# A narrow first slot and a wide second one in an eight-expert layer

## The chip, the cores and the metric

One core of one Trainium2 chip runs the whole program. The metric is device time in microseconds; the kernel before takes 1734.12 us, the median of three runs (1733.98 to 1734.18).

## The reference

Two layers of a diffusion backbone over 256 latent tokens and 256 context tokens, 1024 channels, float32. Layer 0 mixes tokens with a gated chunk MLP and ends with a dense SwiGLU; layer 1 has windowed attention and ends with a mixture of experts. What the change touches is the last of these:

```
logits = xt @ w_router                       # 256 tokens, 8 experts
top_v, top_i = top_k(logits, 2)
gates = sum(one_hot(top_i) * softmax(top_v))
for e in range(8):
    y += gates[:, e:e+1] * ((silu(xt @ w_gate[e]) * (xt @ w_up[e])) @ w_down[e])
```

Each expert has w_gate and w_up of 1024 by 3584 and w_down of 3584 by 1024. The kernel computes an expert only for the tokens that chose it: 512 choices over 8 experts, 64 each on average. The output is the latent stream after a final RMSNorm.

## The kernel before, in words

Layer 0, the attention and the second layer's projections take the first 814 us or so. In the mixture of experts the kernel goes through eight **slots** in a fixed order (`MODES`, line 78). A slot has a mode that sets how many tokens it holds and how PE works on them:

- **L** (wide): 128 places. Weights are split into a high and a low fp32r part and each product is three matmuls (`mm3`, lines 231 to 234): high by high, high by low, low by high. The high part is a cast on ACT (line 168), the low part a subtraction on DVE (line 169), both in `split`.
- **S** (narrow): 64 places. Weights are used raw, as float32; the tokens are the stationary operand, 64 columns wide, so that two matmuls stand side by side on the array (`columns`, line 1500 on; the matmul is line 1504).
- **M** (middle): 96 places in three parts of 32, raw weights, four matmuls side by side (line 1504 too).

Slot 0 always holds expert 0 (its weights are addressed before routing is known); the others are ranked by their token counts, the smallest to the S slots and the largest to the remaining L slot (`SLOTRANK`, and `gating`, line 1313 on). If an expert has more tokens than its slot has places, a block under `tc.If(over > 0)` at the end runs all eight experts again, as L slots, for what is left over.

A slot's weights come in 42 **units** of 1 MiB, in the order of `expert_units`: for four chunks of hidden columns (1024, 1024, 1024, 512) the gate units, the up units, and then the down units of the chunk before, so that a slot's last down units stand among the first chunk of the next slot. `chunk` does gate, SiLU on ACT (line 1685), up, and the product of the two on DVE (line 1688); the next chunk's gate transposes that product (line 1541 for a wide slot, 1555 for a raw one) for its down matmuls.

SP issues all loads in program order (line 179). Each unit has a named buffer, and a load waits until that buffer's previous unit is no longer needed: for a raw unit until PE has read it, for a unit of an L slot until it is split. Nine units go early into tiles that are free before the layer's end (`sg`/`at`, and `ORDER`); then `FILLS` names the next buffers, issued around the attention's output projection, and `stages` (line 1133 on) yields the rest in a cycle: `RAW`, `yh`, `FIRSTS`. `side1` and `yh` drop out of the cycle after unit 40 (`YHU`), because they are needed for the sum of the experts' outputs and for a wide slot's scatter. The split halves go into five tiles in turn, three called `wd` and two of the four called `w` (`Halves.half`); `Halves.take` splits up to five halves (two and a half units) ahead of PE. Only after the last L unit do the three `wd` tiles join the cycle as buffers for raw units.

Beside the matmuls there are small steps, one for each unit taken (`extras`): the routing's `gating`, the gather of the next slot's tokens (`gather` for L, line 1388; `gather_raw`, line 1424), their scatter matrix (`back_raw`, line 1437), and `combine`, which adds a finished slot to the sum (lines 1606 and 1630). The first slot's gather runs before the first chunk, in an order written out by hand. For a wide first slot it alternates DVE and ACT and splits the tokens too (lines 1394 to 1409).

Of the kernel before, what the change touches and what calls it, by code (L numbers as in the profile page):

```python
# [8 lines left out]
def _quiet(msg, *args, **kwargs):  # L9
# [6 lines left out]
F32 = mybir.dt.float32  # L16
F32R = mybir.dt.float32r
I32 = mybir.dt.int32
AF = mybir.ActivationFunctionType
OP = mybir.AluOpType  # L20
# [3 lines left out]
P = 128  # L24
# [12 lines left out]
UNIT = 2048  # L37
# [15 lines left out]
LOOK = 2  # L53
NHALF = 5
HB = 5
FIRSTS = ('wst',) * 3 + ('xgb0', 'side0', 'wx', 'wst3', 'hx', 'side1', 'xgb1')
FILLS = 'wst wst hx0 wst xgb0 side0 wx wst3 hx1 side1'
LH = 5
RAW = ('wsx', 'wst5', 'hc', 'wst2', 'wst4')
ORDER = ('xgb0', 'xgb1', 'wsx', 'wst5', 'hc', 'wst2', 'wst4', 'yh')  # L60
PLACE = ('xgb', 'wst2', 'wst4', 'wst5', 'sg', 'at', 'yh')
TACT = 0, 2
# [8 lines left out]
BEGIN = "v a a n00 w0 s1 c t3 t2 m00 s1 a q3 a q2 W1 f n10 a n01 n11 b m10 a a n21 m01 s1 s1 a n20 n30 n31 a m11 a s1 m21 n41 a n40 m31 a w1 n51 m20 m30 s1 s1 n50 a m40 a n60 s1 s1 a n61 m41 m51 a m50 m60 m61 n70 n71 m71 m70"  # L71
START = {mybir.EngineType.PE, mybir.EngineType.SP}
WARM = 4, 4
YHU = 40
GY = 2
TMM = (3,)

MODES = "LSLMSMMS"
PARTS = {"S": (64, 1), "M": (32, 3)}
SLOTCAP = [P if m == "L" else PARTS[m][0] * PARTS[m][1] for m in MODES]  # L80
SLOTRANK = [-1] + [sum(MODES[1:].count(x) for x in "SML"[:"SML".index(m)]) + MODES[1:s + 1].count(m) - 1
                   for s, m in enumerate(MODES) if s]

# [48 lines left out]
def body(tc, nc, I, out, dbg=None):  # L132
    ctxs = []

    def pool(**kw):
        return tc.tile_pool(**kw)

    V, A, PE = nc.vector, nc.scalar, nc.tensor
# [3 lines left out]
    with top:  # L142
        con = top.enter_context(pool(name="con", bufs=1))
        psp = top.enter_context(pool(name="psum", bufs=1, space=PSUM))
        wst = top.enter_context(pool(name="wst", bufs=3))
        hpool = tc.tile_pool(name="hpool", bufs=1, side="right")
        hp = hpool.__enter__()
        cur = {}
# [3 lines left out]
        def s2t(dt=F32):  # L152
            return ph.tile([P, 512], dt, name="s2", bufs=S2)

        def wtile():
            return ph.tile([P, UNIT], F32R, name="w", bufs=4)
# [4 lines left out]
        def mm_ps(dt=F32):  # L161
            return psp.tile([P, 512], dt, name="mm", bufs=6)

        def tp_ps(dt=F32):
            return psp.tile([P, 512], dt, name="tp", bufs=2)
# [71 lines left out]
        ph = top.enter_context(pool(name="all", bufs=1))  # L237
# [56 lines left out]
        hx = [ph.tile([P, 4, 256], F32, name=f"hx{i}", bufs=1) for i in range(2)]  # L294
        hc = ph.tile([P, DT, 256], F32, name="hc", bufs=1)
# [94 lines left out]
        G = [[con.tile([P, DT, 2], F32, name=f"G{l}{n}") for n in range(2)] for l in range(2)]  # L390
# [128 lines left out]
        def mod(l, i, d, s):  # L519
            return modT[l][:, 8 * i + d, s:s + 1]  # L520
# [131 lines left out]
        first = ada_first()  # L652
# [201 lines left out]
        for g in range(7):  # L854
# [15 lines left out]
            for which in ("g", "u"):  # L870
                if g == 0 and which == "g":
                    u = []
                    ps = []
# [17 lines left out]
                for fh in range(2):  # L891
                    u = stream.take(2)
                    feed(FEED.get((g, which, fh), 1))
                    for f2 in range(2):
                        ps = mm_ps()
# [190 lines left out]
        def expert_units(exs):  # L1086
            last = None
            for ex in exs:
                c0 = 0
                for w in CH:  # L1090
                    k = 2 * 1024 // w
                    for which in ("gate", "up"):
                        for r0 in range(0, D, k * P):
                            yield ex, (which, r0, k, c0, w), (k, w)
                    if last is not None:
                        yield from down_units(*last)
                    last = ex, c0, w
                    c0 += w
            yield from down_units(*last)
# [14 lines left out]

        order = [Expert(m, s, None, None if s else 0) for s, m in enumerate(MODES)]
        first_units = list(expert_units(order))
        units = list(first_units)
        early = {n: mp.tile([P, SIZES.get(n, UNIT)], F32, name=n, bufs=1) for n in PLACE}
# [4 lines left out]
        def source(u):  # L1123
            ex, what, shape = u
            return ex.slice(*what), shape
# [6 lines left out]

        def stages():
            i = len(loaded)
            split_ends = max(j for j, u in enumerate(units) if u[0].mode == "L")
            for n in FIRSTS[FIRSTS.index("side1") + 1:]:
                i += 1
                yield n
            while True:
                for n in RAW + ("yh",) + FIRSTS + (("wd",) * (NHALF - 2) if i > split_ends else ()):  # L1140
                    if n == "wd" and "rest" in cur:
                        continue
                    if n != "wx" and (n not in ("yh", "side1") or i < YHU):
                        i += 1
                        yield n

        stage = stages()

        def moe_load(u):
# [59 lines left out]
        moe_stream = Halves(first_units)  # L1209
# [47 lines left out]
        side = ph.tile([P, 4096], F32, name="side", bufs=1)  # L1257
        early["side0"], early["side1"] = side[:, :UNIT], side[:, UNIT:]
        sums = early["side1"].rearrange("p (c d) -> p c d", c=2)
        early["wx"] = ph.tile([P, UNIT], F32, name="w", bufs=4)  # L1260
        early["hx"] = [ph.tile([P, UNIT // 2], F32, name=f"hx{i}", bufs=1) for i in range(2)]
        fills = FILLS.split()
        split_unit = source(units[len(loaded) + [n for n in fills if n != "hx0"].index("hx1")])
        parts = []
        for n in fills:
            if n[:2] == "hx":
                src, (k, n_) = split_unit
                i = int(n[2])
# [16 lines left out]
        for c in range(2):  # L1285
            V.scalar_tensor_tensor(lg[:, c, :], lgp[:, NE * c:NE * c + NE], rt[:, c:c + 1], wrb[:, 1, :],
                                   op0=OP.mult, op1=OP.add)
# [77 lines left out]
        def one_hot(oh, ex, value, n=P):  # L1365
            for c in range(2):
                V.tensor_scalar(oh[:, c, :], C("iota")[:, :n], ex.arrays[0][:, c, ex.col:ex.col + 1],
                                ex.arrays[value][:, c, ex.col:ex.col + 1], op0=OP.is_equal, op1=OP.mult)

        def gather(ex, first=False):  # L1370
            if ex.mode != "L":
                yield from gather_raw(ex)
                return
            oh = s2t()[:, :2 * P].rearrange("p (c s) -> p c s", c=2)
            one_hot(oh, ex, 2)
            for _ in range(GY):
                yield
            xg = wtile().rearrange("p (i d s) -> p i d s", i=2, d=DT)
            ex.xg = xg
            n = 2 if first else 4  # L1380
            held = []
            for d0 in range(0, DT, n):
                tmp = s2t()[:, :n * P]
                ps = mm_ps() if first and d0 % 4 else tp_ps()
                for a in range(n):
                    for c in range(2):
                        h, d = divmod(d0 + a, 4)
                        PE.matmul(ps[:, a * P:(a + 1) * P], acct[c, h][:, d * P:(d + 1) * P], oh[:, c, :],
                                  start=(c == 0), stop=(c == 1))
                yield  # L1390
                for a in range(n):
                    dst, src, g, b = tmp[:, a * P:(a + 1) * P], ps[:, a * P:(a + 1) * P], G[1][1][:, d0 + a, 0:1], mod(1, 3, d0 + a, 0)
                    if first and a:
                        V.tensor_scalar(dst, src, g, b, op0=OP.mult, op1=OP.add)
                    else:
                        A.activation(dst, src, AF.Identity, bias=b, scale=g)
                tmp = tmp.rearrange("p (d s) -> p d s", s=P)
                A.copy(xg[:, 0, d0:d0 + n, :], tmp)
                held.append((d0, tmp))
                if not first or d0:  # L1400
                    low(xg, *held.pop(0))
                yield
            if first:
                low(xg, *held.pop(0))
                moe_stream.ahead(NHALF)
# [2 lines left out]
            n = tmp.shape[1]  # L1408
            V.tensor_sub(xg[:, 1, d0:d0 + n, :], tmp, xg[:, 0, d0:d0 + n, :])

        def gather_raw(ex):
            n = SLOTCAP[ex.col]
            oh = s2t()[:, :2 * n].rearrange("p (c s) -> p c s", c=2)
            one_hot(oh, ex, 2, n)
            for _ in range(GY):
                yield
            ex.tile = ph.tile([P, UNIT], F32, name="w", bufs=4)
            ex.xg = ex.tile[:, :DT * n].rearrange("p (d s) -> p d s", d=DT)
            for d0 in range(0, DT, 4):
                ps = tp_ps()  # L1420
                for d in range(d0, d0 + 4):
                    for c in range(2):
                        h, i = divmod(d, 4)
                        PE.matmul(ps[:, (d - d0) * n:(d - d0 + 1) * n], acct[c, h][:, i * P:(i + 1) * P], oh[:, c, :],  # L1424
                                  start=(c == 0), stop=(c == 1))
                yield
                scaled_rows(ex, ps, d0, 4, n)

        def back_raw(ex):
            dg = s2t().rearrange("p (a c t) -> p a c t", a=2, c=2)  # L1430
# [13 lines left out]
                V.scalar_tensor_tensor(ex.oht[:, i, :], held[:, :256], C("place" + ex.mode)[:, i:i + 1], held[:, 256:],  # L1444
                                       op0=OP.is_equal, op1=OP.mult)

        def scaled_rows(ex, ps, d0, k, n):
            for d in range(k):
                A.activation(ex.xg[:, d0 + d, :], ps[:, d * n:(d + 1) * n], AF.Identity,
                             bias=mod(1, 3, d0 + d, 0), scale=G[1][1][:, d0 + d, 0:1])  # L1450

        def gather_back(ex):
            if ex.mode != "L":
# [22 lines left out]
        for _ in gather(order[0], True):  # L1476
            pass
# [237 lines left out]
        with tc.manual_schedule(engines=MOE):  # L1715
# [4 lines left out]
            ex = order[-1]  # L1720
            y = scaled(ex)
            ps = {(c, h): tp_ps() if h else mm_ps() for c in range(2) for h in range(2)}
# [8 lines left out]
        with tc.If(over > 0):  # L1731
# [3 lines left out]
            rest = [Expert("L", e, [past, sel, selr, gates], e) for e in range(NE)]  # L1735
# [38 lines left out]
```

## Time and profile before

| | us |
|---|---|
| median of three runs | 1734.12 |
| the profiled execution | 1732.13 |
| its span | 1730.0 |
| PE busy | 1686.2 |
| DVE busy | 887.3 |
| ACT busy | 564.0 |
| bytes moved by DMA | 477.88 MB |

The span is the time from the first to the last instruction of the profiled execution; what lies around it is 2.13 us. Times in the rows below are microseconds from the span's start. A float32 matmul on PE stands in the profile as two records, an fp32r matmul as one. Matmuls overlap, so that the duration of one record is longer than the distance from its start to the next one's; where the pace of PE matters, distances are read.

### The profile page before, as it was taken

The numbers are of one execution on the slowest core, as the hardware profiler recorded it, in microseconds if no ns is written. First come the engines' busy times: TensorE is split into PE (matmuls) and PEld (weight loads), VectorE is DVE, ScalarE is ACT, GpSimd is POOL, SyncE is SP. The second block draws the span as 40 slices with busy tenths as digits, with TensorE's granted clock in tenths as the row PEclk, the third lists the DMA queues.
The fourth block names the chain that finished last, engine by engine and source line by source line (L and its number), as shares of the span: only waits on it lengthen the run. The fifth ranks groups of instructions, "written<-read, shape, count | busy, mean of one in ns | idle before, by whom it ended". The sixth has DMA issues, their size and how long they took to land.

```text
span 1730.0 us, 32514 instructions
## 1 busy us (share of the span) xinstructions
PE 1686.2 (97%) x13735; PEld 1195.5 (69%) x13735; DVE 887.3 (51%) x1638; ACT 564.0 (33%) x1006; POOL 37.2 (2%) x33
## 2 busy tenths in 40 slices
PE   7999999999999999999899999999999999999997
PEld 4678988788787879979787447876654456656532
DVE  5579677767687767786887318862001010020021
ACT  4434532222222234685676126751000001001000
POOL 0000000000000000050000000000000000000000
PEclk9999999999999999999999999999999999999998
DMA  9765345544455432327888999999999999999994
GB/s 309 266 223 191 98 147 195 169 148 153 139 170 189 152 122 98 99 78 284 299 313 298 404 403 409 403 409 408 402 376 405 406 408 402 407 377 345 373 403 170
DMA packets 193736, 477.88 MB, mean 276 GB/s; under 512 B 9096, under 2 KB 68656, under 8 KB 192560
## 3 DMA queue, kind: packets, MB, share of 16 engines
q1 hardware_dynamic: 193584, 475.73, 74.8%
q8 instruction: 110, 1.80, 0.4%
q14 instruction: 42, 0.34, 0.1%
HBM read 474.65 MB, written 1.05 MB: 275 GB/s over the span
## 4 chain that ended last, share of the span: by engine, by line
PE 89%; DVE 4%; DMA 4%; issue 1%; ACT 1%; SPq 1%; POOL 0%; DVEq 0%; ACTq 0%
PE mm L1504 31%; PE mm L232 16%; PE mm L233 16%; PE mm L234 16%; PE tp L1424 1%; PE tp L1606 1%; DMA wst<-in_moe_w_gate_dram 1%; DMA xgb<-in_moe_w_gate_dram 1%; PE mm L1021 1%; PE mm L458 1%; PE tp L1555 1%; DVE wd L169 1%; DVE w L169 1%; DMA wst<-in_ada_w_dram 1%; DMA side<-in_ctx_dram 1%
## 5 line engine op out<-in xcount | busy, mean ns | idle before, releaser
L1688 DVE TENSOR_TENSOR sg<-sg,mm 128x512 f32<-128x512 f32 (+2 forms) x50 | 27.5, 580 | 408.3 <-PE mm L1504 408.3
L232 PE MATMUL mm<-b,w 128*128 128x512 f32 (+1 forms) x560 | 206.2, 368 | 0.0
L233 PE MATMUL mm<-b,w 128*128 128x512 f32 (+1 forms) x560 | 205.0, 366 | 0.0
L234 PE MATMUL mm<-b,w 128*128 128x512 f32 (+1 forms) x560 | 204.7, 366 | 0.0
L169 DVE TENSOR_TENSOR w<-wst,w 128x512 fp32r<-128x512 f32 (+1 forms) x201 | 145.2, 764 | 76.4 <-ACT w L168 76.0
L168 ACT CAST w<-wst 128x512 fp32r<-128x512 f32 (+1 forms) x201 | 127.5, 683 | 173.9 <-PE mm L233 129.8
L1504 PE MATMUL mm<-wst,w 128*32 128x256 f32 (+3 forms) x2544 | 177.1, 373 | 6.6 <-issue 6.6
L494 DVE SCALAR_TENSOR_TENSOR s<-wst,cT,s 128x512 f32<-128x512 f32 x224 | 153.3, 748 | 9.1 <-DMA wst<-in_ada_w_dram 9.1
L1504 PEld LDWEIGHTS mm<-wst,w 128*32 128x32 f32 (+1 forms) x2544 | 90.5, 115 | 79.2 <-issue 49.5
L1557 ACT COPY s<-tp 128x512 f32<-128x512 f32 (+2 forms) x33 | 16.4, 498 | 325.3 <-PE tp L1555 266.3
L232 PEld LDWEIGHTS mm<-b,w 128*128 128x128 f32 x560 | 105.7, 189 | 23.0 <-ACT side L168 4.2
L234 PEld LDWEIGHTS mm<-b,w 128*128 128x128 f32 x560 | 105.6, 189 | 17.0
L233 PEld LDWEIGHTS mm<-b,w 128*128 128x128 f32 x560 | 105.7, 189 | 16.7 <-DVE b L169 0.2
L1504 PE MATMUL mm<-wst,s 128*32 128x256 f32 (+1 forms) x1240 | 93.9, 403 | 1.3 <-issue 0.7
L232 PE MATMUL mm<-b,side 128*128 128x512 f32 (+1 forms) x240 | 90.9, 379 | 0.0
L234 PE MATMUL mm<-b,side 128*128 128x512 f32 (+1 forms) x240 | 90.2, 376 | 0.0
L233 PE MATMUL mm<-b,side 128*128 128x512 f32 (+1 forms) x240 | 90.0, 375 | 0.0
L232 PE MATMUL mm<-w,b 128*128 128x512 f32 (+1 forms) x224 | 79.3, 355 | 0.0
L233 PE MATMUL mm<-w,b 128*128 128x512 f32 (+1 forms) x224 | 78.1, 350 | 0.2 <-DVE w L169 0.2
L234 PE MATMUL mm<-w,b 128*128 128x512 f32 (+1 forms) x224 | 77.9, 348 | 0.0
L1504 PEld LDWEIGHTS mm<-wst,s 128*32 128x32 f32 (+1 forms) x1240 | 45.5, 113 | 45.6 <-issue 22.5
L1685 ACT ACTIVATE sg<-mm 128x512 f32<-128x512 f32 (+2 forms) x50 | 23.6, 510 | 149.8 <-PE mm L1504 149.8
(402 smaller groups left out, 3059.0 us busy)
## 6 DMA issues: line engine op xcount, KB each, us to landing
wst<-in_moe_w_gate_dram SPq DMA_DIRECT2D x55, 1024.0 KB, 13.2
wst<-in_moe_w_up_dram SPq DMA_DIRECT2D x51, 1024.0 KB, 14.1
wst<-in_moe_w_down_dram SPq DMA_DIRECT2D x51, 1024.0 KB, 14.8
wst<-in_ada_w_dram SPq DMA_DIRECT2D x40, 1024.0 KB, 5.2
xgb<-in_moe_w_gate_dram SPq DMA_DIRECT2D x18, 1024.0 KB, 11.7
wst<-in_ffn_w_gate_dram SPq DMA_DIRECT2D x14, 1024.0 KB, 5.0
wst<-in_ffn_w_up_dram SPq DMA_DIRECT2D x14, 1024.0 KB, 5.0
wst<-in_ffn_w_down_dram SPq DMA_DIRECT2D x14, 1024.0 KB, 5.1
```

The source lines that it names most:

```text
L168: A.copy(hi, src)
L169: V.tensor_sub(lo, src, hi)
L232: PE.matmul(ps, sh, mh, start=start, stop=False)
L233: PE.matmul(ps, sh, ml, start=False, stop=False)
L234: cur["pe"] = PE.matmul(ps, sl, mh, start=False, stop=stop).ins
L458: PE.matmul(ps[j:j + 32, :], ones[:, :32], acc_[s], start=True, stop=True)
L494: V.scalar_tensor_tensor(acc_[s], u[:, k, :], c_, acc_[s], op0=OP.mult, op1=OP.add)
L1021: PE.matmul(ps[64 * par:64 * par + 64, :256], vt[:, kc, 64 * kvh:64 * kvh + 64], pT[:, kc, par].rearrange("p a b -> p (a b)"), start=(kc = ...
L1424: PE.matmul(ps[:, (d - d0) * n:(d - d0 + 1) * n], acct[c, h][:, i * P:(i + 1) * P], oh[:, c, :], start=(c == 0), stop=(c == 1))
L1504: PE.matmul(ps[n * g:n * g + n, c0:c0 + w], x, wrow[:, w * g:w * g + w], start=start and first, stop=stop and last)
L1685: A.activation(x, p, AF.Silu)
L1688: V.tensor_mul(x, x, p)
```

## The change

`MODES` goes from `LSLMSMMS` to `SLSMMSMS`: slot 0 (expert 0) is narrow, the one wide slot is second, and the numbers of middle slots (three) and of narrow slots among the others (three) stay. The buffers' order is one list, `CYCLE`. `FILLS` no longer reuses `xgb0`; instead it loads three raw units into the `wd` tiles and one more into a `w` tile (`wy`), so that 21 units instead of 18 and a reused buffer are addressed up to the first cycle. `yh` now leaves the cycle after unit 70, `side1` after unit 40 as before. The raw gather learns the first slot's form: four of its eight scalings go to DVE, and `moe_stream.ahead` is called after it.

```diff
-FIRSTS = ('wst',) * 3 + ('xgb0', 'side0', 'wx', 'wst3', 'hx', 'side1', 'xgb1')
-FILLS = 'wst wst hx0 wst xgb0 side0 wx wst3 hx1 side1'
+CYCLE = ('xgb0', 'xgb1', 'wsx', 'wst5', 'hc', 'wst2', 'wst4', 'yh', 'wst', 'wst', 'wst', 'wd', 'wd', 'wd', 'side0', 'wst3',
+         'hx', 'side1')
+FILLS = 'wst wst hx0 wst wd wd wd side0 wx wy wst3 hx1 side1'
 LH = 5
-RAW = ('wsx', 'wst5', 'hc', 'wst2', 'wst4')
...
-YHU = 40
+LEAVE = {'yh': 70, 'side1': 40}
...
-MODES = "LSLMSMMS"
+MODES = "SLSMMSMS"
...
-            split_ends = max(j for j, u in enumerate(units) if u[0].mode == "L")
-            for n in FIRSTS[FIRSTS.index("side1") + 1:]:
-                i += 1
-                yield n
+            split_ends = max((j for j, u in enumerate(units) if u[0].mode == "L"), default=0)
             while True:
-                for n in RAW + ("yh",) + FIRSTS + (("wd",) * (NHALF - 2) if i > split_ends else ()):
-                    if n == "wd" and "rest" in cur:
+                for n in CYCLE:
+                    if n == "wd" and (i <= split_ends or "rest" in cur):
                         continue
-                    if n != "wx" and (n not in ("yh", "side1") or i < YHU):
+                    if i < LEAVE.get(n, i + 1):
                         i += 1
                         yield n
...
-        early["wx"] = ph.tile([P, UNIT], F32, name="w", bufs=4)
+        for n in ("wx", "wy"):
+            early[n] = ph.tile([P, UNIT], F32, name="w", bufs=4)
...
-                yield from gather_raw(ex)
+                yield from gather_raw(ex, first)
...
-                scaled_rows(ex, ps, d0, 4, n)
+                scaled_rows(ex, ps, d0, 4, n, first)
+            if first:
+                moe_stream.ahead(NHALF)
...
-        def scaled_rows(ex, ps, d0, k, n):
+        def scaled_rows(ex, ps, d0, k, n, first):
             for d in range(k):
-                A.activation(ex.xg[:, d0 + d, :], ps[:, d * n:(d + 1) * n], AF.Identity,
-                             bias=mod(1, 3, d0 + d, 0), scale=G[1][1][:, d0 + d, 0:1])
+                dst, src, g, b = ex.xg[:, d0 + d, :], ps[:, d * n:(d + 1) * n], G[1][1][:, d0 + d, 0:1], mod(1, 3, d0 + d, 0)
+                if first and d % 2 == 0:
+                    V.tensor_scalar(dst, src, g, b, op0=OP.mult, op1=OP.add)
+                else:
+                    A.activation(dst, src, AF.Identity, bias=b, scale=g)
```

## Rows read from the trace of the kernel before

**Rows 1.** The page: rate of DMA in 40 equal slices, and the last chain by engine.

```profile
GB/s 309 266 223 191 98 147 195 169 148 153 139 170 189 152 122 98 99 78 284 299 313 298 404 403 409 403 409 408 402 376 405 406 408 402 407 377 345 373 403 170
...
PE 89%; DVE 4%; DMA 4%; issue 1%; ACT 1%; SPq 1%; POOL 0%; DVEq 0%; ACTq 0%
```

**Rows 2.** Timeline of DVE: one of the 32 products (line 1688) that end a chunk.

```profile
938.20 0.68 DVE L1688 TENSOR_TENSOR sg<-sg,mm 128x512 f32<-128x512 f32 x1
```

**Rows 3.** Windows, slot by slot: length, engines' busy us, PEclk, DMA share, GB/s.

```profile
823.60:938.20 114.60, 110.02 (x513) 91.40 (x512) 99.36 (x118) 86.68 (x101) 0.00 (x0) 0.99 0.89 314
938.20:1025.20 87.00, 87.00 (x442) 40.79 (x443) 19.99 (x31) 16.24 (x28) 0.00 (x0) 1.00 0.95 371
1025.20:1149.30 124.10, 121.58 (x563) 93.33 (x560) 102.28 (x101) 88.41 (x101) 0.00 (x0) 1.00 1.03 407
1149.30:1272.90 123.60, 120.00 (x2051) 78.37 (x2053) 20.42 (x33) 16.73 (x33) 0.00 (x0) 1.00 1.02 402
1272.90:1364.70 91.80, 91.80 (x687) 39.24 (x681) 8.89 (x19) 7.68 (x17) 0.00 (x0) 1.00 1.02 395
1364.70:1486.20 121.50, 117.76 (x2034) 70.79 (x2034) 9.99 (x23) 9.68 (x24) 0.00 (x0) 0.99 1.03 406
1486.20:1612.80 126.60, 124.95 (x2297) 77.58 (x2292) 10.65 (x25) 9.57 (x24) 0.00 (x0) 1.00 0.98 371
1612.80:1704.00 91.20, 90.46 (x658) 36.65 (x652) 11.65 (x29) 5.00 (x9) 0.00 (x0) 1.00 0.99 386
1704.00:1730.00 26.00, 13.49 (x58) 4.29 (x54) 7.60 (x15) 3.26 (x9) 1.54 (x2) 0.83 0.12 44
```

**Rows 4.** Timeline of PE in the first slot: start, duration, line, operands.

```profile
822.89 1.06 PE L1388 MATMUL mm<-s,s 128*128 128x128 f32 x8
823.71 0.47 PE L232 MATMUL mm<-wd,w 128*128 128x512 f32 x1
...
828.37 0.39 PE L232 MATMUL mm<-w 128*128 128x512 f32 x1
...
831.09 0.39 PE L232 MATMUL mm<-wd,w 128*128 128x512 f32 x1
...
850.79 1.11 PE L1541 MATMUL tp<-cst,sg 128*128 128x128 f32 x4 [4.58 <-DVE sg L1688]
```

**Rows 5.** Waits of SP's queue, 700 to 960: us in total, times, longest.

```profile
SPq L179 <- DVE w L169: 81.4, 18, 14.2
```

**Rows 6.** The chain that ended last, 983 to 1057: start, us, what.

```profile
983.71 1.06 PE tp L1437 x2
984.76 7.02 PE mm L1504 x32
991.78 0.59 PE tp L1555 x4
...
995.95 1.98 PE tp L1388 x16
...
1038.35 18.77 DMA wst<-in_moe_w_gate_dram
```

**Rows 7.** Windows: a narrow slot's fourth chunk, the second wide slot's first.

```profile
1010.60:1025.20 14.60, 14.60 (x102) 7.19 (x100) 0.71 (x2) 0.97 (x2) 0.00 (x0) 1.00 1.04 402
1025.20:1059.40 34.20, 32.99 (x146) 21.20 (x142) 20.36 (x18) 19.03 (x21) 0.00 (x0) 1.00 1.02 409
```

**Rows 8.** Timeline of SP's queue: two loads before the first slot.

```profile
804.29 0.37 SPq L179 DMA_DIRECT2D wst<-in_moe_w_gate_dram  x1
...
813.91 0.37 SPq L179 DMA_DIRECT2D side<-in_moe_w_up_dram  x1
```

**Rows 9.** Windows: ten microseconds behind the first wide slot's last chunk.

```profile
940.00:950.00 10.00, 10.00 (x49) 6.84 (x49) 2.97 (x4) 0.87 (x2) 0.00 (x0) 1.00 0.44 167
```

**Rows 10.** SP's last loads, and the median time to landing of their kind.

```profile
1684.27 3.67 SPq L179 DMA_DIRECT2D wst<-in_moe_w_down_dram  x2
...
wst<-in_moe_w_down_dram SPq DMA_DIRECT2D x51, 1024.0 KB, 14.8
```

More of the change, by code (lines that the diff above doesn't have):

```diff
@@ L1409, in low, with gather_raw @@
             V.tensor_sub(xg[:, 1, d0:d0 + n, :], tmp, xg[:, 0, d0:d0 + n, :])
-        def gather_raw(ex):
+        def gather_raw(ex, first):
             n = SLOTCAP[ex.col]
```

## The prediction

> **What bounds the kernel now.** I read the page first, then the mixture-of-experts stage by slot, then single stretches of PE. The page's slices show two halves: from slice 18 on the experts' weights stream in, at 284 to 409 GB/s until the last slice, and the chain that ended last is 89% PE [rows 1]. So PE sets the end, but the load queue is close behind, and which of the two wins has to be settled slot by slot.
>
> The slots are cut where a chunk's last product of gate and up starts on DVE (line 1688; the wide first slot ends at 938.20) [rows 2], and the windows between those cuts give one row per slot [rows 3]. In order: wide 114.6 us (from PE's first expert matmul, 823.71, in rows 4), narrow 87.0, wide 124.1, middle 123.6, narrow 91.8, middle 121.5, middle 126.6, narrow 91.2, tail 26.0. Each slot's weights are 42 units of 1 MiB, 44.04 MB. At the 402 to 409 GB/s of the slots in which the queue runs full, that is about 108.6 us a slot, 2.59 us a unit. A narrow slot is therefore 17 to 22 us quicker on PE than its loads, a wide or middle one 13 to 18 us slower. The first slot differs: DMA 314 GB/s, DVE busy 99 of 115 us, and the queue waited 81.4 us, in 18 waits, for one of the two tiles that DVE's low-part subtraction fills [rows 3, 5]. There the queue waits for the splits and for PE, not PE for the queue.
>
> **The change, part by part.** Expert 0 always takes slot 0. That slot becomes 64 places with raw weights, and the one remaining wide slot comes second. By the reference's own routing on its inputs the experts get 64, 77, 60, 41, 36, 75, 88 and 71 tokens: expert 0 has exactly 64, which fits.
>
> *Start.* PE's gather ran into its first expert matmul without a gap (last eight records from 822.89, matmul at 823.71) [rows 4]. The new gather has as many instructions, of half the columns. If only columns counted it would save about 2 us; the eight records of 1.06 us could as well be held by their weight loads. I take no gain; bounds 0 to -2.
>
> *First slot, narrow in place of wide.* Four units of a narrow slot take PE 7.02 us (1.755 each) [rows 6]. First chunk: 8 units, 14.0, with 0.6 of the gating's small matmuls and hand-over, 14.7. Second: 8 units 14.0, a transpose step 0.6, the gather-back matmul 1.06 [rows 6], and about 0.7 in which PE waits for the product: 16.4. Third: 12 units 21.1, transposes 0.6, the next gather twice 1.98 [rows 6]: 25.6. Fourth: 8 units, which took 14.6 in the other narrow slot [rows 7]. Sum 71.3 us in place of 114.6: **-43.3**. In it goes the 4.58 us hole at 850.79, where PE waited for a product that DVE could not start until the split ahead of it was done [rows 4]. The splits of this slot (84 casts and 84 subtractions, two for each unit) vanish from ACT and DVE, in the projection before it as well; that one is PE-bound, so I count nothing there. The two scalings shared out to DVE have four small operations each and hide behind PE's second half of the gather.
>
> *Wide slot second.* It keeps its 124.1 us save for the first chunk. That took 34.2 [rows 7]: the chain ran through 18.77 us of a load that a split stood waiting for, with the product queued behind the split on DVE [rows 6]. Of PE's own it is 4 narrow units 7.0, transposes 0.6, and 8 wide units of 2.72 (twelve matmuls, 828.37 to 831.09 [rows 4]) 21.8: 29.4. So **-4.8**, if the loads are there in time (below).
>
> *Order of the others.* Before, the middle slots followed a wide, a narrow and a middle one (123.6 + 121.5 + 126.6); after, a narrow, a middle and a narrow one (121.5 + 126.6 + 121.5): **-2.1**. A narrow slot after a wide one stays at 87.0, the one between middles at 91.8, the last at 91.2, the tail at 26.0 [rows 3].
>
> *Loads.* This is where cover could fail. The weight loads now take three split buffers and a second scratch buffer as well, so 21 units are asked for before PE has consumed one, and three buffers are full that splits used before. SP issued the third staging load at 804.29 and the first into the side buffer at 813.91 [rows 8]; three loads of 2.59 us now go between them. From 804 on I expect no gap: unit 12 lands near 811, unit n at 808 + 2.59 (n - 11). PE is through 36 units at 895.0 and the queue then has 45 or 46: 25 us ahead. The wide slot is slower than its loads and adds 11 us (119.3 against 108.6); its cycle has 13 raw buffers, plus 2.5 units already split. At the change from wide to narrow, buffers come free late, because a raw unit is held until PE has read it, a split one only until it is split: before, the rate fell to 167 GB/s there [rows 9]. Over that whole narrow slot the rate was 371 against 406, which is 7.5 us of 87 lost; I take 7 again. The narrow slot then eats 21.6 (87.0 against 108.6), the middle slot's first chunk some 3 more: 25 + 11 - 7 - 21.6 - 3 leaves about 4 us. That is the tightest point, and a thin one. Later slots regain 13 to 18 us each when they are middle ones, and lose 17 when narrow.
>
> *Sum.* -43.3 - 4.8 - 2.1 = -50.2 us on a span of 1730.0: 1679.8. The profiled execution took 1732.13, 2.13 more than its span, and the runs' median is 1734.12, 2.0 above that execution; on that median the forecast is **1683.9**.
>
> **A rule against it.** The rows say that one core here draws 402 to 409 GB/s through whole slots [rows 3]. The Trainium skill (DMA: Bandwidth & Descriptors, Where 436 GB/s comes from) holds that transfers out of HBM bind at about 358 GB/s for a core; by that the 324 units still to come at 804 would last 949 us and the kernel would end past 1770, slower than now. The trace is above that figure in every slot but the first, by 12% and more in three, so the measurement decides.
>
> **The rivals.** *The load queue sets the end.* In every slot but the first, DMA is at 371 GB/s or more, and no byte is saved. The queue then ends where it began plus its bytes: 324 units from 808 on are 839 us, 1647, plus what it lost in these slots before (7.5 us in the narrow slot after the wide one, 2.5, 11, 4.5 in the later ones, worked out from their rates against 406, and 1 in the first middle slot: 26.5), and 27 from the last landing to the end (last issue done at 1687.9, a median of 14.8 us to landing [rows 10], end at 1730): 1701 span, 1705 on the median. For it: the slack of 4 us. Against: losses in the middle slots come from full buffers, when the queue is far ahead, and cost nothing. The Trainium skill (Perfetto Trace Analysis, Identifying the Most-Contended Engine) would call DMA the most contended engine here, by its share of HBM bandwidth, and expect little from taking work off PE. The chain's 89% PE speaks otherwise.
>
> A milder form: only the tight point fails, and the middle slot starts 4 to 12 us late: 1688 to 1696.
>
> *A 65th token: slower.* If the kernel's own routing gave expert 0 one place more than 64, the condition behind the eight slots holds and all eight experts run again as wide slots for the overflow. Eight slots at the wide slot's 124.1 us are 993 us: about 2680. It decides at one token. In the reference the closest third choice for expert 0 lies 0.016 in the logits behind the second, and the split products keep far more digits than that. The slot's rows cannot show a count, hence a small chance.
>
> *The change does not do what it says*: the split buffers, still full of raw units, hold up the first splits of the wide slot. It would be seen as a stall at 895 to 925, priced at twice the 4.8 us that waiting splits cost the wide slot's first chunk before: 1694.
>
> **How the numbers follow.** PE-bound as summed 0.62; queue-bound at the tight point or held-up splits 0.22; queue-bound throughout 0.12; overflow 0.03; and 0.01 for a load queue slower than any row shows. The forecast's own spread is about 10 us down (2 at the start, 1.7 to 3.7 for PE short of busy in each of the three middle slots [rows 3], which may not recur), so 1674; upward the range takes in the milder cases and most of the queue-bound one, 1704. This kernel's measurement can tell about 0.2% from no change, 3.5 us. So faster 0.95, same 0.01, slower 0.04.
>
> **What would show it.** Right: the first slot about 71 us long at 400 GB/s or more; no waits on split tiles before 895; the second slot's first chunk near 29 us; the other slots as now. Wrong: a first middle chunk over 30 us with a load in the chain (the tight point), DMA at 400 throughout with PE idle in middle slots (queue-bound), a second pass after the eighth slot (overflow).

## The result and the profile after

The changed kernel takes 1685.28 us, the median of four runs (1684.53 to 1689.36), against 1734.15 for the kernel before on the same chip: a ratio of 0.9723, with a 95% interval of 0.9706 to 0.974. The forecast was 1683.9. The profiled execution took 1684.53 us and its span is 1682.4.

The page of the changed kernel first, the lines that answer to [rows 1]:

```profile
GB/s 310 281 223 180 123 126 200 150 153 158 140 175 169 181 151 101 76 88 211 361 388 409 409 387 358 404 408 408 402 407 406 393 369 403 408 408 402 407 404 222
...
PE 91%; DMA 4%; DVE 2%; issue 1%; ACT 1%; POOL 0%; SPq 0%; DVEq 0%; ACTq 0%
```

The four slices near 300 GB/s in [rows 1], 18 to 21 counted from 0, are gone: from slice 20 the queue moves 388 or more in all but four slices. PE's share of the chain rose from 89 to 91%, DVE's fell from 4 to 2%. DMA's share stayed at 4%, and that share turns out to be the one to watch.

Windows by slot, cut where a chunk's product starts on DVE (now line 1691), against [rows 3] and with the same columns. The order is narrow, wide, narrow, middle, middle, narrow, middle, narrow, tail:

```profile
823.30:894.70 71.40, 70.55 (x373) 28.30 (x374) 10.04 (x32) 13.98 (x25) 0.00 (x0) 1.00 1.01 393
894.70:1015.70 121.00, 121.00 (x563) 93.36 (x560) 102.96 (x102) 86.08 (x98) 0.00 (x0) 1.00 1.02 401
1015.70:1102.60 86.90, 86.90 (x442) 40.83 (x443) 18.57 (x29) 14.68 (x26) 0.00 (x0) 1.00 0.99 382
1102.60:1224.20 121.60, 116.69 (x2037) 69.27 (x2037) 9.95 (x23) 9.70 (x24) 0.00 (x0) 1.00 1.03 406
1224.20:1354.10 129.90, 125.29 (x2293) 77.55 (x2289) 10.63 (x24) 9.59 (x24) 0.00 (x0) 1.00 1.01 397
1354.10:1445.90 91.80, 91.80 (x686) 41.78 (x680) 8.89 (x19) 7.69 (x17) 0.00 (x0) 1.00 1.02 396
1445.90:1565.60 119.70, 116.19 (x2035) 69.27 (x2035) 9.97 (x23) 9.49 (x24) 0.00 (x0) 1.00 1.03 406
1565.60:1656.40 90.80, 90.22 (x659) 36.74 (x652) 11.62 (x29) 5.00 (x9) 0.00 (x0) 1.00 1.03 405
1656.40:1682.40 26.00, 13.51 (x58) 4.29 (x54) 7.60 (x15) 3.26 (x9) 1.54 (x2) 0.87 0.29 111
```

In the first slot DVE fell from 99.36 us busy to 10.04, and the slot from 114.6 us to 71.4. All others are within 3.3 us of a slot of the kernel before with the same neighbour.

The start, on PE:

```profile
819.64 3.68 PE L1422 MATMUL tp<-s,s 128*128 128x64 f32 x32
823.25 1.08 PE L1507 MATMUL mm<-sg,w 128*64 128x512 f32 x4
```

And the chain that ended last: from the first expert matmul on it runs through a load in two pieces only (start, us, what):

```profile
1091.81 18.40 DMA wsx<-in_moe_w_gate_dram
...
1115.12 18.05 DMA wd<-in_moe_w_down_dram
```

The two stops of PE that belong to them, from its timeline (in brackets the idle time before the instruction and what ended it):

```profile
1110.25 2.80 PE L1507 MATMUL mm<-wsx,w 128*32 128x256 f32 x48 [0.25 <-DMA wsx<-in_moe_w_gate_dram]
...
1133.21 1.94 PE L1507 MATMUL mm<-wd,s 128*64 128x512 f32 x8 [0.17 <-DMA wd<-in_moe_w_down_dram]
```

PE stood still for 0.25 and 0.17 us, at the place that the prediction had called the tightest. The chain gives DMA 36 us for it. A chain names what came last, however small the margin; the idle time in brackets is what the wait cost. Two loads at full length in the chain, and 0.42 us of idle time, say that here PE and the queue arrived almost together.

### The profile page after: what moved, and what is told of

It is laid out like the page before. It is cut to its first block, busy times and chain, and to the rows that moved or that the text cites. A ratio compares the mean times of both kernels' runs of the same rounds, so it can differ in the third digit from the quotient of the medians.

```text
span 1682.4 us, 31904 instructions
## 1 busy us (share of the span) xinstructions
PE 1640.8 (98%) x13581; PEld 1124.5 (67%) x13581; DVE 781.5 (46%) x1540; ACT 475.1 (28%) x910; POOL 37.2 (2%) x33
## 4 chain that ended last, share of the span: by engine, by line
PE 91%; DMA 4%; DVE 2%; issue 1%; ACT 1%; POOL 0%; SPq 0%; DVEq 0%; ACTq 0%
PE mm L1507 35%; PE mm L232 15%; PE mm L233 15%; PE mm L234 15%; PE tp L1422 2%; PE tp L1609 1%; DMA wsx<-in_moe_w_gate_dram 1%; DMA wd<-in_moe_w_down_dram 1%; PE tp L1558 1%; PE mm L1021 1%; PE mm L458 1%; DMA side<-in_ctx_dram 1%; PE tp L1006 1%; PE tp L1437 0%; DMA wst<-in_ada_w_dram 0%
## 5 line engine op out<-in xcount | busy, mean ns | idle before, releaser
L1691 DVE TENSOR_TENSOR sg<-sg,mm 128x512 f32<-128x512 f32 (+2 forms) x47 | 25.6, 569 | 491.7 <-PE mm L1507 489.2
L1507 PE MATMUL mm<-wst,w 128*32 128x256 f32 (+3 forms) x2528 | 192.3, 386 | 6.8 <-issue 6.8
L168 ACT CAST w<-wst 128x512 fp32r<-128x512 f32 (+1 forms) x186 | 111.9, 653 | 171.5 <-PE mm L233 129.6
L169 DVE TENSOR_TENSOR w<-wst,w 128x512 fp32r<-128x512 f32 (+1 forms) x186 | 127.1, 727 | 63.8 <-ACT w L168 63.2
L1560 ACT COPY s<-tp 128x512 f32<-128x512 f32 (+2 forms) x37 | 18.6, 503 | 383.3 <-PE tp L1558 324.3
L1507 PE MATMUL mm<-wd,w 128*32 128x256 f32 (+2 forms) x864 | 70.6, 404 | 0.1
```

The source lines that it names most:

```text
L168: A.copy(hi, src)
L169: V.tensor_sub(lo, src, hi)
L1507: PE.matmul(ps[n * g:n * g + n, c0:c0 + w], x, wrow[:, w * g:w * g + w], start=start and first, stop=stop and last)
L1560: A.copy(dst, pt[:, :len(bs) * P])
L1691: V.tensor_mul(x, x, p)
```

## The experiments

My theory was the prediction's: PE's work sets the end, and the extra early loads only keep the queue out of the way. The rivals were that the gain comes from raw weights and earlier loads, and that the load queue sets the end. Nine kernels test them. Each is the changed kernel with one edit, and each was run beside runs of the kernel before; a ratio below is to those.

**The narrow slot or the raw weights.** The first slot becomes a middle one: raw weights, early loads and order stay, PE's work is about a wide slot's.

```diff
-MODES = "SLSMMSMS"
+MODES = "MLSMMSMS"
```

> The first slot in the middle mode (96 places, raw weights) in place of the narrow one, the rest of the changed kernel as it is: raw weights, all buffers and order, but PE's work about that of a wide slot. If the gain is PE's work in a narrow slot: the first slot takes about 106 us in place of 71.5, the wide slot behind it some 5 more for a middle slot's scatter and down units, 1722 to 1728. If the gain came from raw weights and the earlier loads, most of it stays: 1690 to 1700.

Measured: 1733.46 us, a ratio of 0.9998 (0.9989 to 1.0008) to the kernel before. The whole gain is gone. First and second slot, in windows:

```profile
823.30:931.70 108.40, 104.64 (x1988) 66.59 (x1991) 12.29 (x39) 18.17 (x34) 0.00 (x0) 1.00 0.85 309
931.70:1061.60 129.90, 129.90 (x821) 104.90 (x814) 103.87 (x103) 84.70 (x96) 0.00 (x0) 1.00 0.89 336
```

The first slot costs 37.0 us more than the narrow one and the wide slot behind it 8.9 more, for the middle slot's down units and scatter. DVE has as little to do as in the changed kernel (12.29 us of 108), and still there is no gain: raw weights alone give nothing, the narrow slot's shorter work on PE gives all of it. The expected 1722 to 1728 was too low by 5: the wide slot took 8.9 more, not 5, and the first slot 108.4, not 106. The queue moved 309 GB/s here, much like the 314 of [rows 3]. What the queue waited for in the first slot (us in total, times, longest), in this kernel (823 to 932) and then in the kernel before (823 to 940):

```profile
SPq L179 <- PE mm L1507: 82.7, 28, 12.6
...
SPq L179 <- DVE wd L169: 60.9, 22, 7.2
SPq L179 <- DVE w L169: 27.6, 13, 3.8
```

So a slow queue in a first slot is no sign of splits by itself: without them the queue waits about as long for PE to read the raw units.

**The early loads.** The four loads that the change added to `FILLS` (three `wd` and `wy`) are left out.

```diff
-FILLS = 'wst wst hx0 wst wd wd wd side0 wx wy wst3 hx1 side1'
+FILLS = 'wst wst hx0 wst side0 wx wst3 hx1 side1'
```

> The changed kernel, but the four extra early loads (three into the split tiles, one into the second scratch tile) are left out: 17 units are asked for early in place of 21. PE alone: PE's work is the same and it never waited, so 1685 within 1 us. PE with the load queue close behind: the queue runs dry at about 819 and can go on only when PE frees the first buffer near 828, so it is 8 us later for good; at the tight point (the first middle slot's first chunk, now 28.3 us) there is no slack left, so that chunk becomes 35 to 38 us and the whole 1692 to 1695.

Measured: 1694.21 us, ratio 0.9766 (0.975 to 0.9782), 7 to 9 us above the changed kernel. Windows: ten microseconds at the start, the fourth chunk of the narrow slot behind the wide one, and the first chunk of the middle slot behind that:

```profile
804.00:814.00 10.00, 10.00 (x84) 9.87 (x84) 2.94 (x7) 1.25 (x3) 0.00 (x0) 1.00 0.35 120
1089.20:1107.80 18.60, 15.26 (x100) 6.57 (x96) 0.70 (x2) 0.97 (x2) 0.00 (x0) 1.00 1.04 396
1107.80:1139.20 31.40, 28.79 (x418) 14.47 (x418) 0.45 (x2) 1.24 (x3) 0.00 (x0) 1.00 1.02 408
```

The same three stretches of the changed kernel:

```profile
804.00:814.00 10.00, 10.00 (x85) 9.87 (x85) 2.89 (x8) 1.09 (x4) 0.00 (x0) 1.00 0.98 378
1088.00:1102.60 14.60, 14.60 (x102) 7.20 (x100) 0.73 (x2) 0.97 (x2) 0.00 (x0) 1.00 1.04 399
1102.60:1130.90 28.30, 27.95 (x418) 14.37 (x414) 0.40 (x2) 1.24 (x3) 0.00 (x0) 1.00 1.03 408
```

At 804 to 814 the queue moved 120 GB/s where the changed kernel moves 378, and 280 us later PE pays for it: 18.6 us in place of 14.6, and 31.4 in place of 28.3. The gap lay at 804 to 814 more than behind 819, where I had looked for it, and the wait is spread over two chunks, but the size is the one expected. So the early loads are no gain by themselves (the middle first slot had them too) and some 8 us of loss if they are missing: the narrow slots use up the lead.

**Where the wide slot stands.** It goes third, behind two narrow slots. The edit also swaps the fifth slot and the sixth, which come after the stretch that is read here.

```diff
-MODES = "SLSMMSMS"
+MODES = "SSLMSMMS"
```

> Order narrow, narrow, wide, middle, narrow, middle, middle, narrow: the wide slot third, nothing else changed. PE alone: the slots' own times, with the transitions as they were seen, sum to about 2.5 us more, 1688. With the load queue: after one narrow slot the queue is 25 us ahead, the second narrow slot eats 22, and the wide slot wants its units 2.5 early for the splits; so its first chunk takes 34 to 38 us in place of 28.3 and the whole is 1692 to 1698.

Measured: 1698.48 us, ratio 0.9797 (0.9783 to 0.981), 13 us above the changed kernel. The second narrow slot and the wide slot's first chunk:

```profile
894.80:985.60 90.80, 84.76 (x424) 30.48 (x420) 9.55 (x19) 9.14 (x19) 0.00 (x0) 1.00 1.03 406
985.60:1024.20 38.60, 34.07 (x140) 22.08 (x142) 20.53 (x18) 19.12 (x21) 0.00 (x0) 0.96 1.03 410
```

The queue is full throughout, at 406 and 410 GB/s, and PE is short of busy by 6.0 and 4.5 us. The chunk took 38.6 us, just above what was expected (34 to 38), and so did the whole (1692 to 1698); that PE would wait within the second narrow slot already was not expected. Two narrow slots in a row use their loads faster than the queue brings them.

**No two narrow slots near each other.** The third and the fourth slot change places.

```diff
-MODES = "SLSMMSMS"
+MODES = "SLMSMSMS"
```

> Order narrow, wide, middle, narrow, middle, narrow, middle, narrow: no two narrow slots close together, no tight point. PE alone: the slots' times sum to within 1 us of the changed kernel's, 1684 to 1686. With the load queue ahead all the way, the 0.6 us of the tight point goes as well: 1683 to 1686. If loads set the end throughout, the same bytes give the same time; a gain of over 4 us would say that the queue costs more in the changed kernel than the 0.6 us.

Measured: 1690.72 us, ratio 0.9752 (0.9739 to 0.9765), 5 us above the changed kernel, with intervals that just touch: a miss. The middle slot behind the wide one, and the tail:

```profile
1015.90:1140.20 124.30, 121.69 (x2051) 80.16 (x2053) 20.41 (x33) 16.60 (x33) 0.00 (x0) 0.99 0.94 366
...
1657.10:1687.80 30.70, 14.76 (x58) 4.23 (x58) 7.61 (x15) 3.26 (x9) 1.54 (x2) 0.86 0.43 169
```

PE in the last down units, what the queue waited for in the slot behind the wide one (us in total, times, longest), and its last issue:

```profile
1658.51 1.94 PE L1507 MATMUL mm<-xgb,s 128*64 128x512 f32 x8 [1.57 <-DMA xgb<-in_moe_w_down_dram]
...
SPq L179 <- PE mm L1507: 61.8, 26, 7.1
...
1653.22 2.10 SPq L179 DMA_DIRECT2D wst<-in_moe_w_down_dram  x1
```

Up to 1657 the kernel is level with the changed one (1656.4). Then its tail takes 30.7 us in place of 26.0, because PE waits for most of the last loads; the very last was issued at 1653.22, where the changed kernel issues it at 1647.01. Behind the wide slot the queue fell to 366 GB/s for 124 us, with full buffers: it waited for PE to read raw units. Nobody waited for the queue there. At 406 GB/s those bytes would have taken 12 us less; the changed kernel loses some 6 less than this one over its slots (from their rates against 406), and that is by how much the last issue is late. "Costs nothing while the queue is ahead" holds only if the queue stays ahead to the last byte.

**Less work on PE in the first slot.** In slot 0 every second row of a unit gets no matmul (in `gate_up`, shown, and likewise with `f` in `down`); half of that expert's products are left out, and all loads stay:

```diff
+HALVED = 0
...
+                    if ex.col == HALVED:
+                        if k % 2:
+                            continue
+                        stop = k == DT - 2
...
```

> Every second row of each unit is left out of the matmuls of the first slot (half of expert 0's products are not computed), 37 us of PE; loads as before. PE alone: 1648. With the load queue close behind: the queue ran at 390 to 412 GB/s from 804 on already and cannot go faster, so PE waits in the slots behind; the tight point stays where it is and the whole gains 0 to 4 us: 1681 to 1685.

Measured: 1678.75 us, ratio 0.968 (0.9665 to 0.9695): about 7 us gained of 37. The first three slots in windows:

```profile
823.30:872.50 49.20, 41.72 (x212) 16.40 (x211) 10.05 (x32) 10.77 (x21) 0.00 (x0) 0.98 1.03 404
872.50:1000.90 128.40, 123.01 (x539) 93.84 (x540) 102.75 (x101) 88.77 (x101) 0.00 (x0) 0.94 1.03 407
1000.90:1090.00 89.10, 87.43 (x441) 40.32 (x439) 18.55 (x28) 14.71 (x26) 0.00 (x0) 1.00 1.03 406
```

The queue runs at 404 to 407 GB/s through all three and PE waits. The gain lies above the expected 0 to 4. The rates tell why: with PE close behind, the queue gains not only in the first slot (404 for 393) but in the wide slot and the narrow one behind it too (407 and 406 for 401 and 382), which together is worth some 9 us of loading. Of PE's 37 us, 30 were given back.

**Less work on PE late.** The same edit for the sixth slot.

```diff
-HALVED = 0
+HALVED = 5
```

> Every second row of each unit is left out of the matmuls of the sixth slot (the narrow one between two middle ones; half of one expert's products are not computed), 37 us of PE; loads as before. PE alone: 1648. With the load queue just behind PE: in the changed kernel the last down units landed about 2 us before PE read them, and the queue ran at 396 GB/s or more from the middle slots on; so the queue has 2 us to give at the end and the 3 to 5 us that full buffers cost it in the fifth and sixth slot: 1678 to 1683.

Measured: 1684.24 us, ratio 0.9713 (0.9698 to 0.9728), not to be told from the changed kernel's 0.9723 (0.9706 to 0.974). The sixth slot and the two behind it:

```profile
1354.90:1432.10 77.20, 67.01 (x524) 30.05 (x516) 8.86 (x19) 7.68 (x17) 0.00 (x0) 0.93 1.01 393
1432.10:1558.00 125.90, 117.54 (x2007) 70.60 (x2008) 9.96 (x23) 9.47 (x24) 0.00 (x0) 0.95 1.03 406
1558.00:1651.30 93.30, 90.75 (x657) 36.72 (x652) 11.57 (x28) 5.00 (x9) 0.00 (x0) 1.00 1.03 406
```

The sixth slot is 14.6 us shorter, not 37, then the middle slot is 6.2 longer, the last 2.5 and the tail 4.7 (30.7 from 1651.3 to the end at 1682.0, for 26.0): the queue allows no more. While PE waited for loads its granted clock fell: 0.93 and 0.95 of full speed in the mean of the first two windows, so for a part of them at the lower of its two levels. How much of the time given back lies there was not separated; but the queue ran at 406 GB/s in the last two windows, and a faster PE would have waited for it. The time came out 1 us above the expected range. The reason can be read in the changed kernel: the last down unit but one (`hc`) was issued at 1644.38, took 17.9 us to land, so until 1662.3, and PE read it at 1664.00; the last unit was issued at 1647.01, took 17.8, so until 1664.8, and PE read it at 1665.77. Their issues, from the timeline of SP's queue:

```profile
1644.38 2.17 SPq L179 DMA_DIRECT2D hc<-in_moe_w_down_dram  x1
1647.01 2.06 SPq L179 DMA_DIRECT2D wst<-in_moe_w_down_dram  x1
```

Their landings, from the view of the tile `hc` from 1640 on and of `wst` from 1646 on:

```profile
DMA to landing us min/median/max: 17.9/17.9/17.9
...
DMA to landing us min/median/max: 17.8/17.8/17.8
```

Their first matmuls, from the timeline of PE:

```profile
1664.00 1.94 PE L1507 MATMUL mm<-hc,s 128*64 128x512 f32 x8 [0.52 <-ACT s L1560]
1665.77 1.89 PE L1507 MATMUL mm<-wst,s 128*64 128x512 f32 x8
```

One to two us are all the slack that is left. In the changed kernel PE and the queue finish together.

**The last wide slot.** The largest expert has 88 tokens, so a middle slot would hold it.

```diff
-MODES = "SLSMMSMS"
+MODES = "SMSMMSMS"
```

> The one wide slot replaced by a middle one (the largest expert has 88 tokens, 96 places hold it): no split of expert weights at all, and the three split tiles serve raw units from the start. PE alone: a middle slot after a narrow one took 121.6 us, the wide one 121.0; but a narrow slot after a middle one took 91.8 where it took 86.9 after the wide one: 5 us more, 1689 to 1692. If the splits or the buffers they hold still cost time in the changed kernel, this is faster than it: 1675 to 1684.

Measured: 1688.95 us, ratio 0.9745 (0.9729 to 0.9761), by the medians some 4 us slower; the two intervals overlap, but the windows show the same 4 us. Second and third slot:

```profile
894.70:1015.70 121.00, 117.40 (x2054) 69.97 (x2054) 10.55 (x24) 9.47 (x24) 0.00 (x0) 1.00 1.03 405
1015.70:1107.00 91.30, 90.94 (x669) 39.05 (x663) 8.26 (x17) 7.68 (x17) 0.00 (x0) 1.00 1.02 398
```

A middle slot takes the wide one's 121.0 us, and the narrow slot behind it 4.4 more than 86.9. The queue does better (405 and 398 GB/s for 401 and 382), DVE is at 10.55 us for 102.96, and no load is in the chain of this stage any more; none of that helps while PE has 4 us more to do. It agrees with PE's sum, at the low edge of the expected range.

**The scalings on ACT.** In `scaled_rows`:

```diff
-                if first and d % 2 == 0:
+                if False:
```

> All eight scalings of the first gather on ACT again, none on DVE. The first expert matmul waits for the gather's own second half on PE, which ends 1.8 us after the first half; the first half's four scalings take about 1.5 us on one engine. So no more than 0.5 us: 1685 to 1686. If the scalings stood on the path, the four that move would add 1.0 to 1.5 us.

Measured: 1685.95 us, ratio 0.9723 (0.971 to 0.9736): the same as the changed kernel. ACT does four scalings in 1.29 us:

```profile
821.43 1.29 ACT L1453 ACTIVATE w<-tp,modT,G 128x64 f32<-128x64 f32 x4 [1.98 <-PE tp L1422]
```

They end at 822.7, and the first expert matmul of this kernel starts at 823.11, when PE has finished its gather. Sharing them out changed nothing.

**One token too many.** In `constants`:

```diff
-    add("slotcap", np.broadcast_to(np.array(SLOTCAP)[None, :], (P, NE)))
+    add("slotcap", np.broadcast_to(np.array([SLOTCAP[0] - 1] + SLOTCAP[1:])[None, :], (P, NE)))
```

> The capacity that the kernel compares with is 63 places for the first slot, though it still takes 64: expert 0's last token counts as overflow, and is added once more. This prices a 65th token. All eight experts run again as wide slots: eight times the wide slot's 121 us is 968, plus a start from an empty queue of 10 to 20 us and a tail: 2650 to 2700. If the second pass were cheap for lack of tokens, it would stay under 1800; its products do not depend on how many places are filled.

Measured, in one run: 2699.94 us, at the top of the expected range. A window over nearly all of the second pass:

```profile
1720.00:2690.00 970.00, 964.70 (x4479) 799.51 (x4477) 885.05 (x883) 752.47 (x861) 0.00 (x0) 1.00 0.93 347
```

PE is busy for 964.70 of 970 us, with no fewer matmuls for a pass that has one token to add. So the narrow first slot is fast for inputs in which expert 0 has at most 64 tokens, and the kernel is 1015 us slower from the 65th on. These inputs have exactly 64.

## Why the prediction was right

*First slot: right.* 71.3 us were summed, 71.4 measured; its later three chunks were put at 16.4, 25.6 and 14.6 and measured 16.6, 25.5 and 14.6. That PE's work is the cause, not the splits, is shown by the middle first slot, which has no splits either and gains nothing. One row was misread on the way: the 81.4 us of waits in [rows 5] cover 700 to 960, and most of them lie before the slot. Within it the queue waited 60.9 and 27.6 us for the split tiles (the lines stand with the middle first slot above), so the conclusion stays. One sign missed by a little: the slot was to run at 400 GB/s or more and ran at 393.

*Start: right to take no gain.* The gather's 32 records with 64 columns took 3.6 us from the first to the matmul behind them; with 128 columns they had taken 3.5, from here to 823.71 [rows 4]:

```profile
820.22 1.05 PE L1388 MATMUL tp<-s,s 128*128 128x128 f32 x8
```

The gather itself began 0.6 us sooner (819.64), and so PE began with the experts 0.5 us sooner all the same.

*Wide slot: 1.7 us off.* -4.8 was expected of its first chunk, which took 28.3 in place of 29.4, so 5.9 us less than before. But its second took 32.3 where it had taken 29.5. The changed kernel's two chunks, and the second one of the kernel before:

```profile
894.70:923.00 28.30, 28.30 (x128) 19.93 (x125) 20.62 (x18) 18.16 (x20) 0.00 (x0) 1.00 1.03 409
923.00:955.30 32.30, 32.30 (x145) 22.84 (x145) 29.78 (x32) 20.98 (x24) 0.00 (x0) 1.00 1.03 409
...
1059.40:1088.90 29.50, 28.18 (x125) 21.57 (x126) 29.45 (x34) 22.15 (x24) 0.00 (x0) 1.00 1.03 409
```

Before, the cut between the two, a product on DVE, was itself late, and PE had already begun the next chunk: the first window holds 146 of PE's records before and 128 after, the second 125 and 145. So part of the 34.2 in [rows 7] was the second chunk's. Both together went from 63.7 to 60.6, and the whole slot from 124.1 to 121.0: -3.1. PE had been idle for 2.5 us of the 63.7, which is about what could be gained; the 18.77 us of the chain in [rows 6] was the length of a load, not of a wait. A cut on an engine that is late moves time between its neighbours; the term should have been taken over both.

*The other slots: right in sum.* The middle slots were put at 121.5 + 126.6 + 121.5 and took 121.6 + 129.9 + 119.7, 1.6 us more in sum. Two errors partly cancel there: the fourth chunk of the fifth slot took 27.2 for 24.5, that of the seventh 26.4 for 28.2, and in both PE stops on its own account ("issue" in the profile). The narrow ones and the tail came out within 0.4 us each. The span is 1682.4 for 1679.8.

*Loads: the tight point was found, its slack was not.* Four microseconds were expected to be left at the first middle slot's first chunk. PE waited there for 0.42 us in all, and the kernel without the four early loads paid 7 to 9 us, most of it at this point and in the chunk before. Some of the miss is arithmetic: by the prediction's own formula the queue stands at unit 44.6 at 895.0, not at 45 or 46, so 22 us ahead and not 25, and not quite 2 us would have been left. And there was a second tight point, which it did not look for: the last loads, 1 to 2 us ahead of PE. That the queue was just fast enough at both places was luck as much as forecast: the sum of PE's work was right to 2.6 us, and a queue later by a few us would have broken it.

*One argument failed, though the number did not need it:* that the queue's losses behind full buffers "cost nothing". They cost 5 us with the middle slot behind the wide one. The queue was put at 1647 for its last landing if it ran without a gap, and its last unit landed at 1664.8. So the rival in which the load queue sets the end was less far off than its 0.12 said: not the case in this order, in which PE reads the last loads 1 to 2 us behind their landing, but the case as soon as much is taken from PE (37 us for nothing that can be measured late, 37 us for about 7 early). The rival's price of 1705 was too high on two counts: the changed kernel's last load landed 18 us behind that 1647 and not 26.5, and the end came 17.6 us behind the last landing and not 27, a figure that held PE's own lag. The rule of 358 GB/s for a core (the Trainium skill, DMA: Bandwidth & Descriptors, Where 436 GB/s comes from) does not hold here: 401 to 406 stands in four of the slots after, too.

## What to carry to other kernels

Cut a long stage into stretches by kind and neighbour, and a reordering can be summed from stretches already in the trace; take the cuts on the engine that sets the pace. Where two resources are within a few per cent of each other, keep a running lead of one over the other, to the last byte: what a full buffer costs shows far behind it. And a mode chosen for one set of inputs needs the price of the input that does not fit stated beside its gain: here 49 us against 1015.

## What the runs showed that I had not expected

The balance: 37 us less matmul time in one slot is worth nothing that can be measured late and about 7 us early, while PE reads as 98% busy in the page. And PE's own stops in the middle slots' fourth chunk: the same instructions took from 23.5 to 27.9 us in the kernel without a wide slot. What PE waits for there was not tried and stays open.

```profile
PE mm L1507 <- issue: 13.0, 8, 2.5
```

This line of the changed kernel's waits (823 to 1680) puts them at 13.0 us in eight stops, the longest 2.5.
